# Expert results added to one row per token in DRAM, instead of two rows that are summed at the end

## The chip, the cores and the metric

The kernel runs on one core of a Trainium2 chip. The metric is the device time of one execution in microseconds (us). A core has five engines that run their own instruction streams and meet at semaphores: PE (TensorE, the matmuls; PEld is its weight load), DVE (VectorE), ACT (ScalarE), POOL (GpSimd) and SP (SyncE, which here only issues transfers). Transfers between DRAM and the on-chip memory are issued by SP, ACT or POOL and carried out by 16 DMA engines that all of them share; a transfer whose rows are picked by a list of indices (an indirect DMA) is issued by POOL.

## What is computed

The program is one layer of a decoder for 512 prompt tokens and 8 sample tokens (520 in all, 1024 features), in f32. Only its last two steps matter here: a mixture of experts, where every token goes to 2 of 32 experts, and a last RMSNorm over the residual row plus the gated sum of the two experts' outputs.

```python
def finish_layer(...):
    x = x + mods[2] * mix
    h = rmsnorm(x, norm2_g) * (1.0 + mods[4]) + mods[3]
    return x + mods[5] * hier_moe(h, ...)

# hier_moe: top-1 of 4 groups, top-2 of its 8 experts
hid = silu(einsum('nd,edf->nef', hf, w_gate)) * einsum('nd,edf->nef', hf, w_up)
y = einsum('nef,ne,efd->nd', hid, combine, w_down)
# ... and after the layer: y_prompt = rmsnorm(x, final_g)
```

## The kernel before

The program is written once, straight through; a framework turns each engine's part into one fixed instruction stream and puts in the semaphore waits that the data needs. Within an engine everything goes in order, so an instruction that waits holds back what stands behind it.

**Routing.** After the output projection each token's residual row `x1` is written to the DRAM tensor `xrow` (line 1257) and its normed row to `hrow` (line 1282). The routing code then sorts the token-expert pairs into blocks of 64 rows that share one expert. There are 36 regular blocks (`OV0`), two for each of the four fullest experts (`HV`) and one for each of the others, and 16 spare blocks (from line 1683) that this input does not need. It leaves, for every block, the list of rows to fetch (`gix`, one list for a pair of blocks), the row numbers to write to (`six`) and the weights (`wtb`).

**The block loop** (`run`, `turned`, `up`, `hidden`, `flip`, `down`). POOL gathers the rows of a pair of blocks from `hrow` into `xg` (two buffers, line 1585). PE transposes them, multiplies by the expert's gate and up weights (`pgu`, line 1608), ACT and DVE make the hidden row (`hd`, lines 1613 and 1614), PE turns it (`hTp`, line 1620) and multiplies by the down weights (`pd`, line 1629). DVE scales the result by the token's weight and the gate row into `ot`, 128 partitions by 512 (two halves of 64 rows; lines 1632 and 1633; four buffers). POOL then scatters `ot` to `yrow` with an indirect DMA (line 1634); partitions that hold no token have a row number past the end and are left out. SP streams the experts' weights, 3 MB for each, through 21 pages, which hold seven experts (line 1574). The first six experts are loaded ahead.

`yrow` has four half rows for each token, one pair for each of its two experts. No two scatters write the same row, and the program says so, so that no scatter waits for another:

```python
st = G.indirect_dma_start(out=yrow[:, :], out_offset=...six[:, b:b + 1]..., in_=ot, in_offset=None,
                          bounds_check=4 * NT - 1, oob_is_err=False)
for o in scat:
    tc.declare_no_dep(st.ins, o.ins, reason="rows of other slots")
scat.append(st)
```

**The end.** While the last blocks run, SP loads `xrow` back (`xt`, 2 MB, line 1680). After the last scatter it loads `yrow` (`yt`, eight transfers of 512 KB, line 1696, and four small ones for the sample tokens, `ysq`, line 1699). For each of four tiles of 128 tokens, DVE adds the first expert's half to `x` and then the second's (lines 1705 and 1709), ACT sums the squares (line 1710), POOL takes the power -1/2 (line 1716), DVE scales (line 1728) and SP writes the tile out (line 1729). The 8 sample tokens go a way of their own through POOL (`sample`, lines 1732 to 1734, and `quarter_rstd`, line 336) and leave by four transfers from ACT's queue (line 1746).

Of the kernel before, what the change touches and what calls it, by code (L numbers as in the profile page):

```python
# [24 lines left out]
NF = 6  # L25
# [4 lines left out]
GF_ = ()  # L30
ORD, ISS = "t0 t1 f0 t2 f1 s t3 q f2 f3", "fsq"
GT, TH, TF = (), (1, 1, 1, 2), (1, 1, 1, 2)
# [59 lines left out]
def _route():  # L92
# [7 lines left out]
    f = {"dmask": (p < NE - NF)[:, None], "half": (p // 64)[:, None] + 4 * BIG, "valid": (p < NB)[:, None],  # L100
# [80 lines left out]
def body(tc, I, O, dbg=lambda *a: None):  # L181
# [898 lines left out]
    xrow = dr.tile([SEQ, 1024], F32, name="xrow")  # L1080
    yrow = dr.tile([4 * NT, 512], F32, name="yrow")
# [142 lines left out]
    def new_rows():  # L1224
        V.tensor_scalar(pqs[:, 0], pqs[:, 0], ra[:, 0, 4:5], None, op0=ALU.mult)
# [24 lines left out]
    def project(i, n):  # L1250
# [6 lines left out]
        SP.dma_start(xrow[128 * i:128 * i + 128, 512 * n:512 * n + 512], xh)  # L1257
# [405 lines left out]
    pgus, hds, hTs_, scat = {}, {}, {}, []  # L1663
# [24 lines left out]
    ry = yrow.rearrange("(t a) f -> t (a f)", a=4)  # L1688
    ssf = cp.tile([128, 8], F32, name="ssf")
    rsf = cp.tile([128, 8], F32, name="rsf")  # L1690
    ysq = mid("ysq").rearrange("p (a f) -> p a f", a=2)
    V.memset(ysq, 0.0)
    yt = [page(f"yt{i}") for i in range(4)]
    for i in range(4):
        for j in range(2):
            SP.dma_start(half(yt[i], j), ry[128 * i:128 * i + 128, 1024 * j:1024 * j + 1024])  # L1696
        if i == 1:
            for q in range(4):
                SP.dma_start(ysq[32 * q:32 * q + 8].rearrange("p a (c j) -> p (a c) j", c=8),  # L1699
                             ry[512:520].rearrange("b (x r j) -> b x r j", r=4, j=32)[:, :, q])  # L1700
    fs = small("fs")

    def total(i):
        t, t1, x = half(yt[i], 0), half(yt[i], 1), half(xt[i // 2], i % 2)
        (G if i in GT else V).tensor_tensor(x, x, t, op=ALU.add)
        n = 1024 // TH[i]
        for h in range(TH[i]):
            c = slice(n * h, n * h + n)
            op = V.tensor_tensor(t[:, c], x[:, c], t1[:, c], op=ALU.add)  # L1709
            S.activation(t1[:, c], t[:, c], AF.Square, scale=1.0 / 32, accum_out=ssf[:, 2 * i + h:2 * i + h + 1])  # L1710
        r = rsf[:, i:i + 1]
        if TH[i] == 2:
            V.scalar_tensor_tensor(r, ssf[:, 2 * i:2 * i + 1], EPS, ssf[:, 2 * i + 1:2 * i + 2], op0=ALU.add, op1=ALU.add)
        else:
            V.tensor_scalar(r, ssf[:, 2 * i:2 * i + 1], EPS, None, op0=ALU.add)
        G.tensor_tensor(r, r, mh[:, 0:1], op=ALU.pow)  # L1716
        return op

    def final(i):
        n = 1024 // TF[i]  # L1720
        for h in range(TF[i]):
            c = slice(n * h, n * h + n)
            t = half(yt[i], 0)[:, c]
            if i in GF_:
                S.activation(t, t, AF.Copy, scale=rsf[:, i:i + 1])
                G.tensor_tensor(t, t, gfb[:, c], op=ALU.mult)
            else:
                V.scalar_tensor_tensor(t, t, rsf[:, i:i + 1], gfb[:, c], op0=ALU.mult, op1=ALU.mult)  # L1728
            SP.dma_start(O[0][0, 128 * i:128 * i + 128, c], t)

    def sample():
        G.tensor_tensor(fs, ysq[:, 0], ysq[:, 1], op=ALU.add)  # L1732
        G.tensor_tensor(fs, fs, m5s, op=ALU.mult)  # L1733
        G.tensor_tensor(fs, fs, x1s, op=ALU.add)  # L1734

    op = None
    for nm in ORD.split():
        with tc.issue_after(op.ins) if op is not None and nm[0] in ISS else ExitStack():
            r = (sample() if nm == "s" else quarter_rstd(rsf[:, 4:5], fs, 1.0 / D, EPS) if nm == "q" else
                 total(int(nm[1])) if nm[0] == "t" else final(int(nm[1])))  # L1740
        if nm[0] == "t":
            op = r
# [27 lines left out]
```

## Time and profile before

| | |
|---|---|
| median of 3 runs | 810.88 us (805.48 to 825.68) |
| the profiled execution | 803.52 us |
| its span in the trace | 801.7 us |
| block loop, first to last scatter's issue | 537.1 to 765.1 us |
| the end, from the first load of `yrow` | 769.9 to 801.7 us |
| DMA moved in all | 200.02 MB, 249 GB/s on average |

The span is the time from the first to the last instruction in the trace; 1.8 us of the profiled execution lie outside it. Busy shares are averages over the whole span; what a change in the block loop or in the end is worth has to be read in that stretch. A row of the timeline gives start and duration in us, the engine (SPq, ACTq, POOLq are sequencers, which only issue), the line, what is written and read, and in brackets how long the engine was idle before and what ended that.

### The profile page before, as it was taken

How to read it: one execution, taken by the hardware profiler on the slowest of the kernel's cores; microseconds unless marked ns; L12 is line 12 of the kernel's file. 1: busy time of each engine (PE TensorE's matmuls, PEld its weight loads, DVE VectorE, ACT ScalarE, POOL GpSimd, SP SyncE). 2: the span in 40 equal slices, each digit the busy share in tenths (PEclk: the TensorE clock that was granted, in tenths of full speed). 3: DMA queues.
4: the chain of work that ended last, by engine and by line, in shares of the span. 5: the costliest groups of instructions: out<-in, count | busy, mean ns of one | idle time of the engine just before them, and what ended most of it. 6: DMA issues, size and time to landing. Idle time of an engine off the chain costs nothing. (4 is left out here: it accounts for less than half of the span.)

```text
span 801.7 us, 12644 instructions
## 1 busy us (share of the span) xinstructions
PE 697.0 (87%) x4888; PEld 422.2 (53%) x4888; DVE 445.0 (56%) x960; ACT 214.2 (27%) x491; POOL 210.0 (26%) x182
## 2 busy tenths in 40 slices
PE   4999798997989998999999996199999999988800
PEld 3555787876767456544444553155555555545400
DVE  3444729999972868652377668833333334333235
ACT  1254721211122447643335333011011110001011
POOL 5134305043022101014361234212322222311104
PEclk9999999998988999999998999589999999999965
DMA  9975325644958502520015578479999999999653
GB/s 346 421 312 204 140 81 212 239 168 179 335 219 336 242 2 85 218 105 1 0 36 228 194 260 304 153 292 420 418 398 344 419 418 417 417 419 416 261 170 153
DMA packets 42332, 200.02 MB, mean 249 GB/s; under 512 B 10733, under 2 KB 14205, under 8 KB 22677
## 3 DMA queue, kind: packets, MB, share of 16 engines
q1 hardware_dynamic: 29341, 156.27, 50.2%
q0 software_dynamic: 10336, 40.95, 13.2%
q10 hardware_dynamic: 2592, 1.95, 0.8%
q8 instruction: 40, 0.66, 0.3%
q14 instruction: 23, 0.19, 0.1%
HBM read 187.82 MB, written 22.15 MB: 262 GB/s over the span
## 5 line engine op out<-in xcount | busy, mean ns | idle before, releaser
L591 DVE SCALAR_TENSOR_TENSOR y<-u,c,y 128x511 f32<-128x511 f32 (+23 forms) x120 | 103.7, 895 | 2.1
L1634 POOL DMA_INDIRECT yrow<-ot,six x36 | 39.5, 1098 | 107.1 <-DVE ot L1633 99.0
L1613 ACT ACTIVATE hd<-pgu 64x256 f32<-64x256 f32 x36 | 13.5, 375 | 201.1 <-PE pgu L1608 201.1
L1608 PE MATMUL pgu<-eg,mB 128*64 128x256 f32 x256 | 61.5, 383 | 0.0
L1629 PE MATMUL pd<-ed,hTe 128*64 128x512 f32 x240 | 60.3, 600 | 0.4 <-DVE hTe L225 0.4
L1608 PE MATMUL pgu<-eu,mB 128*64 128x256 f32 x256 | 60.3, 382 | 0.0
L1633 DVE SCALAR_TENSOR_TENSOR ot<-pd,wtb,mt 128x512 f32<-128x512 f32 x36 | 27.0, 751 | 54.9 <-PE pd L1629 54.9
L1608 PE MATMUL pgu<-eg,mA 128*64 128x256 f32 x224 | 53.8, 383 | 0.0
L1608 PE MATMUL pgu<-eu,mA 128*64 128x256 f32 x224 | 52.9, 382 | 0.0
L1614 DVE TENSOR_TENSOR hd<-pgu,hd 64x256 f32<-64x256 f32 x36 | 15.4, 428 | 64.8 <-ACT hd L1613 64.8
L1608 PEld LDWEIGHTS pgu<-eg,mB 128*64 128x64 f32 x256 | 33.3, 137 | 21.3 <-issue 6.4
L1608 PEld LDWEIGHTS pgu<-eg,mA 128*64 128x64 f32 x224 | 29.2, 137 | 18.6 <-issue 5.9
L1367 DVE TENSOR_REDUCE ast<-pSp 128x1 f32<-128x384 f32 (+3 forms) x44 | 26.9, 632 | 19.9 <-PE pSp L1364 19.7
L1372 ACT ACTIVATE P<-pSp,ast 128x128 f32<-128x128 f32 (+3 forms) x64 | 33.0, 528 | 15.3 <-DVE ast L1367 13.5
L370 PE MATMUL pr<-cTs,wc 128*64 128x256 f32 x256 | 37.1, 400 | 0.0
L1608 PEld LDWEIGHTS pgu<-eu,mB 128*64 128x64 f32 x256 | 33.8, 137 | 0.8
L1253 PE MATMUL woA<-wo,qT 128*128 128x512 f32 x64 | 32.1, 606 | 0.0
L1109 PE MATMUL woC<-wo,y 128*128 128x512 f32 x64 | 31.2, 605 | 0.0
L361 PE MATMUL cT<-CI,cR 128*128 128x128 f32 x128 | 21.1, 302 | 10.8 <-DVE cR L386 10.7
L1391 PE MATMUL oT<-PTp,kv 128*64 128x512 f32 x80 | 30.2, 618 | 0.0
L225 DVE COPY hTe<-hTp 128x128 f32<-128x128 f32 x36 | 10.5, 291 | 35.0 <-PE hTp L1620 33.7
L1608 PEld LDWEIGHTS pgu<-eu,mA 128*64 128x64 f32 x224 | 29.0, 137 | 0.6
(572 smaller groups left out, 1677.3 us busy)
## 6 DMA issues: line engine op xcount, KB each, us to landing
eg<-in_WG SPq DMA_DIRECT2D x26, 1024.0 KB
eu<-in_WU SPq DMA_DIRECT2D x26, 1024.0 KB
ed<-in_WD SPq DMA_DIRECT2D x26, 1024.0 KB
wada<-in_WA SPq DMA_DIRECT2D x16, 1024.0 KB
wada<-in_WA POOLq DMA_DIRECT2D x8, 1024.0 KB
WG<-in_WG SPq DMA_DIRECT2D x6, 1024.0 KB
WU<-in_WU SPq DMA_DIRECT2D x6, 1024.0 KB
WD<-in_WD SPq DMA_DIRECT2D x6, 1024.0 KB
```

The lines of the kernel that those rows point to most:

```text
L361: PE.transpose(p[:, j, :], R[b:b + n, c, k, 2 * s8:2 * s8 + 2, :], ident[b:b + n, b:b + n])
L370: mark["PE"] = PE.matmul(self.pr[r][64 * c:64 * c + 64], wc1[:, c, 8 * r + 4 * h + s, :], self.T[h][:, c, s], start=(h == 0 and s == 0), s ...
L591: V.scalar_tensor_tensor(yb[:, s_:CVS], ub[:, :CVS - s_], w(k), yb[:, s_:CVS], op0=ALU.mult, op1=ALU.add)
L1109: PE.matmul(p, zc[:, g, 128 * i:128 * i + 128], wo[2 * n + 1][:, g], start=(g == 0), stop=(g == 3))
L1253: PE.matmul(pA, oTp[:, g, 128 * i:128 * i + 128], wo[2 * n][:, g], start=(g == 0), stop=(g == 3))
L1367: V.tensor_reduce(st[k][:, 0, h0:h0 + nh], pS[k][:, :nh * L].rearrange("p (h l) -> p h l", h=nh), axis=AX.X, op=ALU.max, negate=True)
L1372: S.activation(P[k][:, g, :L], pS[k][:, o:o + L], AF.Exp, bias=st[k][:, 0, g:g + 1], accum_out=st[k][:, 1, g:g + 1])
L1391: PE.matmul(oT[64 * k:64 * k + 64, :], kv12[:, br - 1, kt, 128 + 64 * k:192 + 64 * k], PT[k], start=(br == 1 and kt == 0), stop=False)
L1608: PE.matmul(pgus[b][64 * h:64 * h + 64, :], xT[:, c, 64 * s_:64 * s_ + 64], w[:, c, :], start=(c == 0), stop=(c == 7))
L1629: PE.matmul(pd[64 * h:64 * h + 64, :], hT_[:, c, :], wd[:, c, 512 * h:512 * h + 512], start=(c == 0), stop=(c == 1))
L1633: V.scalar_tensor_tensor(ot, pd, wtb[:, b:b + 1], mt, op0=ALU.mult, op1=ALU.mult)
L1634: st = G.indirect_dma_start(out=yrow[:, :], out_offset=bass.IndirectOffsetOnAxis(ap=six[:, b:b + 1], axis=0), in_=ot, in_offset=None, boun ...
```

## The change

`yrow` gets one row of 1024 (two half rows) for each token. The residual row `x1` is written there directly, in place of `xrow`; the eight sample rows, which keep their residual on the chip, are zeroed. Every block's scatter now adds to the rows (`compute_op=ALU.add`). Two blocks can hold the same token, so the declaration that scatters do not depend on each other is gone, and each scatter waits until the last one has landed. At the end four transfers of 512 KB bring finished sums; the loads of `xt` and both additions on DVE are gone. The routing loses five small matmuls and one DVE operation (the slot's part of the row number). The sample tokens' sums move from POOL to DVE, and the last tile's power -1/2 from POOL to ACT's square root with one Newton step on DVE.

```diff
-    xrow = dr.tile([SEQ, 1024], F32, name="xrow")
-    yrow = dr.tile([4 * NT, 512], F32, name="yrow")
+    yrow = dr.tile([2 * NT, 512], F32, name="yrow")
+    ry = yrow.rearrange("(t a) f -> t (a f)", a=2)
...
+        zr = mid("zr")
+        V.memset(zr[:16], 0.0)
+        SP.dma_start(yrow[2 * SEQ:], zr[:16])
...
-        SP.dma_start(xrow[128 * i:128 * i + 128, 512 * n:512 * n + 512], xh)
+        SP.dma_start(ry[128 * i:128 * i + 128, 512 * n:512 * n + 512], xh)
...
-    for a in range(5):
-        PE.matmul(pb[:, 1, :], Rs[:, a, 1], BO[:, 0, 2 * a + 1], start=(a == 0), stop=(a == 4))
-    t6 = box(NBLK)
-    V.tensor_scalar(t6, pb[:, 1], 2.0, K("half"), op0=ALU.mult, op1=ALU.add)
-    V.scalar_tensor_tensor(six, pb[:, 0], 4.0, t6, op0=ALU.mult, op1=ALU.add)
+    V.tensor_scalar(six, pb[:, 0], 2.0, K("half"), op0=ALU.mult, op1=ALU.add)
...
-        st = G.indirect_dma_start(out=yrow[:, :], out_offset=bass.IndirectOffsetOnAxis(ap=six[:, b:b + 1], axis=0), in_=ot, in_offset=None,
-                                  bounds_check=4 * NT - 1, oob_is_err=False)
-        for o in scat:
-            tc.declare_no_dep(st.ins, o.ins, reason="rows of other slots")
-        scat.append(st)
+        G.indirect_dma_start(out=yrow[:, :], out_offset=bass.IndirectOffsetOnAxis(ap=six[:, b:b + 1], axis=0), in_=ot, in_offset=None,
+                             bounds_check=2 * NT - 1, oob_is_err=False, compute_op=ALU.add)
...
-    for i in range(4):
-        SP.dma_start(half(xt[i // 2], i % 2), xrow[128 * i:128 * i + 128])
...
     for i in range(4):
-        for j in range(2):
-            SP.dma_start(half(yt[i], j), ry[128 * i:128 * i + 128, 1024 * j:1024 * j + 1024])
+        SP.dma_start(yt[i], ry[128 * i:128 * i + 128])
...
     def total(i):
-        t, t1, x = half(yt[i], 0), half(yt[i], 1), half(xt[i // 2], i % 2)
-        (G if i in GT else V).tensor_tensor(x, x, t, op=ALU.add)
...
+        S.activation(jy, yt[i], AF.Square, scale=1.0 / 32, accum_out=s_)
+        V.tensor_scalar(s_, s_, EPS, None, op0=ALU.add)
+        if i < 3:
+            G.tensor_tensor(r, s_, mh[:, 0:1], op=ALU.pow)
+            return
+
+        t = e2.tile([128, 2], F32, name="rt2", tag="st")
+        S.activation(t[:, 0:1], s_, AF.Sqrt)
+        V.reciprocal(t[:, 1:2], t[:, 0:1])
...
+    S.activation(rsf[:, 5:6], one, AF.Sqrt)
+    for i in range(4):
+        total(i)
+        final(i)
+        if i == 1:
+            V.tensor_tensor(fs, ysq, m5s, op=ALU.mult)
+            V.tensor_tensor(fs, fs, x1s, op=ALU.add)
+            quarter_rstd(rsf[:, 4:5], fs, 1.0 / D, EPS)
```

POOL's stream in the middle of the block loop, with what each transfer waits for (`DMASW` is the landing of an earlier transfer of POOL's, `PE` and `DVE` an instruction of these engines). Before:

```order
L1585 DMA mA_3288<-hrow_2861,gix_4518 128x1024 [waits DMASW6_49,DMASW4_49,PE_49]
L1634 DMA yrow_2863<-ot_5351,six_4519 2080x512 [waits DMASW5_49,DVE_49]
L1634 DMA yrow_2863<-ot_5402,six_4519 2080x512 [waits DVE_49]
L1585 DMA mB_3289<-hrow_2861,gix_4518 128x1024 [waits DMASW7_49,DMASW1_49,PE_49]
L1634 DMA yrow_2863<-ot_5456,six_4519 2080x512 [waits DMASW0_49,DVE_49]
L1634 DMA yrow_2863<-ot_5507,six_4519 2080x512 [waits DVE_49]
```

The same place now:

```order
L1583 DMA mA_3287<-hrow_2861,gix_4520 128x1024 [waits DMASW6_49,PE_49]
L1633 DMA yrow_2862<-ot_5347,six_4521 1040x512 [waits DMASW3_49,DVE_49]
L1633 DMA yrow_2862<-ot_5398,six_4521 1040x512 [waits DMASW5_49,DVE_49]
L1583 DMA mB_3288<-hrow_2861,gix_4520 128x1024 [waits DMASW1_49,PE_49]
L1633 DMA yrow_2862<-ot_5452,six_4521 1040x512 [waits DMASW6_49,DVE_49]
L1633 DMA yrow_2862<-ot_5503,six_4521 1040x512 [waits DMASW0_49,DVE_49]
```

The order is the same: a gather, then two scatters. POOL's eight landing semaphores (`DMASW0` to `DMASW7`) are taken in turn; what a scatter waited for before was a transfer eight places back, and is now the scatter just ahead of it.

DVE's stream at the end, before (the branch is the jump past the spare blocks):

```order
L1683 UNCONDITIONAL_BRANCH x2
L1692 MEMSET ysq 128x512
L1705 TENSOR_TENSOR xt_6415<-xt_6415,yt_7282 128x1024
L1709 TENSOR_TENSOR yt_7282<-xt_6415,yt_7282 128x1024
L1705 TENSOR_TENSOR xt_6415<-xt_6415,yt_7283 128x1024
L1715 TENSOR_SCALAR rsf<-ssf 128x1
L1709 TENSOR_TENSOR yt_7283<-xt_6415,yt_7283 128x1024
L1728 SCALAR_TENSOR_TENSOR yt_7282<-yt_7282,rsf,gf 128x1024
```

And now:

```order
L1676 UNCONDITIONAL_BRANCH x2
L1684 MEMSET ysq 128x256
L1698 TENSOR_SCALAR ssf<-ssf 128x1
L1714 SCALAR_TENSOR_TENSOR yt_7272<-yt_7272,rsf,gf 128x1024
L1698 TENSOR_SCALAR ssf<-ssf 128x1
L1722 TENSOR_TENSOR fs<-ysq,m5s 128x256
L1714 SCALAR_TENSOR_TENSOR yt_7272<-yt_7272,rsf,gf 128x1024
L1723 TENSOR_TENSOR fs<-fs,x1s 128x256
```

Between two tiles' scaling (line 1714) nothing but a tile's small addition and the sample tokens' two operations is left; the additions of lines 1705 and 1709 are gone.

ACT's stream at the end, now:

```order
L1697 ACTIVATE jy,ssf<-yt_7273 128x1024
L538 ACTIVATE jks,st<-fs 128x256
L1697 ACTIVATE jy,ssf<-yt_7273 128x1024
L1704 ACT_TABLE_LOAD
L1704 ACTIVATE rt_7312<-ssf 128x1
L1728 DMA out<-fs 64x1x32 x4
```

The square root of line 1717, which stands ahead of the loop over the tiles in the code, went to the very start of ACT's stream, so that a table load stands at the end all the same, ahead of the last tile's root and of the sample tokens' four transfers.

## Rows read from the trace of the kernel before

**Rows 1.** The page: each engine's busy time in the whole span.
```profile
PE 697.0 (87%) x4888; PEld 422.2 (53%) x4888; DVE 445.0 (56%) x960; ACT 214.2 (27%) x491; POOL 210.0 (26%) x182
```

**Rows 2.** Windows: start:end, length, each engine's busy us (instructions), PE clock, DMA share, GB/s.
```profile
530.00:595.00 65.00, 65.00 (x474) 34.10 (x472) 23.19 (x46) 6.74 (x15) 16.34 (x15) 1.00 1.01 412
595.00:620.00 25.00, 25.00 (x186) 13.02 (x184) 9.08 (x18) 2.69 (x6) 6.57 (x6) 1.00 0.92 346
620.00:690.00 70.00, 69.27 (x494) 36.11 (x492) 25.20 (x50) 7.71 (x17) 18.04 (x17) 1.00 1.02 418
690.00:745.00 55.00, 48.41 (x352) 27.52 (x350) 18.18 (x34) 5.01 (x11) 11.10 (x11) 1.00 1.00 412
745.00:770.00 25.00, 15.86 (x108) 8.09 (x103) 5.50 (x11) 1.12 (x3) 3.84 (x4) 0.96 0.44 168
770.00:802.00 32.00, 0.59 (x2) 0.50 (x2) 17.13 (x21) 5.18 (x12) 9.66 (x8) 0.50 0.58 200
```

**Rows 3.** Waits, 500 to 802 us: us in total, times, longest us.
```profile
PEld pgu L1608 <- DMA ed<-in_WD: 0.5, 2, 0.3
POOL yrow L1634 <- DVE ot L1633: 99.0, 22, 6.9
```

**Rows 4.** Timeline of POOL in the block loop.
```profile
537.07 1.03 POOL L1634 DMA_INDIRECT yrow<-ot,six  x1 [0.30 <-DVE mt L1632]
...
587.78 1.00 POOL L1634 DMA_INDIRECT yrow<-ot,six  x1 [0.30 <-issue]
592.90 1.16 POOL L1634 DMA_INDIRECT yrow<-ot,six  x1 [4.12 <-DVE ot L1633]
...
600.43 1.00 POOL L1634 DMA_INDIRECT yrow<-ot,six  x1 [0.30 <-issue]
...
729.68 1.16 POOL L1634 DMA_INDIRECT yrow<-ot,six  x1 [6.89 <-DVE ot L1633]
...
765.11 0.98 POOL L1634 DMA_INDIRECT yrow<-ot,six  x1 [5.89 <-DVE ot L1633]
```

**Rows 5.** DMA queues, 730.9 to 734 us (q1: SP's, q0: POOL's): packets, MB, share.
```profile
q1 hardware_dynamic: 180, 1.30, 100.9%
```

**Rows 6.** DMA queues, 734 to 736.3 us.
```profile
q1 hardware_dynamic: 105, 0.77, 79.5%
q0 software_dynamic: 80, 0.24, 25.7%
```

**Rows 7.** DMA queues, 766.6 to 767.2 us.
```profile
q0 software_dynamic: 80, 0.03, 19.7%
```

**Rows 8.** Timeline of the end, all engines.
```profile
769.85 1.74 SPq L1696 DMA_DIRECT2D yt<-yrow  x4
771.91 2.90 SPq L1699 DMA_DIRECT2D ysq<-yrow  x4
773.98 1.23 DVE L1705 TENSOR_TENSOR xt<-xt,yt 128x1024 f32<-128x1024 f32 x1 [3.26 <-DMA yt<-yrow]
...
776.50 1.06 ACT L1710 ACTIVATE yt<-yt 128x1024 f32<-128x1024 f32 x1 [15.63 <-DVE yt L1709]
...
780.48 1.28 DVE L1728 SCALAR_TENSOR_TENSOR yt<-yt,rsf,gf 128x1024 f32<-128x1024 f32 x1
...
789.89 0.15 DVE L1715 TENSOR_SCALAR rsf<-ssf 128x1 f32<-128x1 f32 x1 [2.19 <-ACT yt L1710]
...
790.12 0.95 POOL L1716 TENSOR_TENSOR rsf<-rsf,mh 128x1 f32<-128x1 f32 x1 [1.85 <-DVE rsf L1715]
...
793.48 1.42 DVE L1728 SCALAR_TENSOR_TENSOR yt<-yt,rsf,gf 128x512 f32<-128x512 f32 x2
793.48 3.43 ACTq L1746 DMA_DIRECT2D out<-fs  x4
```

**Rows 9.** Timeline of routing and of the loop's start.
```profile
516.43 0.27 DVE L1514 TENSOR_SCALAR rt<-ptb,RC 128x52 f32<-128x52 f32 x1
...
523.20 1.28 ACT L1613 ACT_TABLE_LOAD   x1
```

More of the change, by code (lines that the diff above doesn't have):

```diff
@@ L29 @@
 KTE = "VSSSSVVSSSSSSSVSSSSVVSSS"
-GF_ = ()
-ORD, ISS = "t0 t1 f0 t2 f1 s t3 q f2 f3", "fsq"
-GT, TH, TF = (), (1, 1, 1, 2), (1, 1, 1, 2)
+TF = (1, 1, 1, 2)
 PLAN = ",c0,spread gn im sel,,,c1,k0 n cp,,,mc,,sn n3 n1 n0 n2,k1 rw,,,nq,,,,,,,,,,,,,cs,"
@@ L99, in _route @@
          "eio": full(np.arange(32)), "rev": full(64 - np.arange(32)), "thr": full(64 * np.arange(1, 9))}
-    f = {"dmask": (p < NE - NF)[:, None], "half": (p // 64)[:, None] + 4 * BIG, "valid": (p < NB)[:, None],
+    f = {"dmask": (p < NE - NF)[:, None], "half": (p // 64)[:, None] + 2 * BIG, "valid": (p < NB)[:, None],
          "inv": np.where(p < NB, 0, -1000)[:, None], "ti": full(128 * (np.arange(10) // 2) - BIG)}
@@ L1661, in run @@
         down(*before)
-    pgus, hds, hTs_, scat = {}, {}, {}, []
+    pgus, hds, hTs_ = {}, {}, {}
     asked = {0, OV0 // 2, NBLK // 2}
@@ L1677, in body @@
     SP.dma_start(gfb, I["GF"])
-    xt = [page("xt0"), page("xt1")]
-    for i in range(4):
-        SP.dma_start(half(xt[i // 2], i % 2), xrow[128 * i:128 * i + 128])
     spare = [[page(f"sg{j}"), page(f"su{j}"), page(f"sd{j}")] for j in range(3)]
@@ L1685, in body @@
         run([(b, lambda b=b: left(b - OV0)) for b in range(OV0, NBLK)], asked)
-    ry = yrow.rearrange("(t a) f -> t (a f)", a=4)
     ssf = cp.tile([128, 8], F32, name="ssf")
     rsf = cp.tile([128, 8], F32, name="rsf")
-    ysq = mid("ysq").rearrange("p (a f) -> p a f", a=2)
+    ysq = small("ysq")
     V.memset(ysq, 0.0)
-    yt = [page(f"yt{i}") for i in range(4)]
+    yt = [half(p, j) for p in (page("yt0"), page("yt1")) for j in range(2)]
+    jy = page("jy")[:, 0:1024]
     for i in range(4):
-        for j in range(2):
-            SP.dma_start(half(yt[i], j), ry[128 * i:128 * i + 128, 1024 * j:1024 * j + 1024])
+        SP.dma_start(yt[i], ry[128 * i:128 * i + 128])
@@ L1697, in body @@
         if i == 1:
             for q in range(4):
-                SP.dma_start(ysq[32 * q:32 * q + 8].rearrange("p a (c j) -> p (a c) j", c=8),
-                             ry[512:520].rearrange("b (x r j) -> b x r j", r=4, j=32)[:, :, q])
+                SP.dma_start(ysq[32 * q:32 * q + 8].rearrange("p (c j) -> p c j", c=8),
+                             ry[512:520].rearrange("b (c r j) -> b c r j", r=4, j=32)[:, :, q])
     fs = small("fs")
     def total(i):
-        t, t1, x = half(yt[i], 0), half(yt[i], 1), half(xt[i // 2], i % 2)
@@ L1705, in total @@
-        (G if i in GT else V).tensor_tensor(x, x, t, op=ALU.add)
[L1706 to L1715, printed above, removed]
@@ L1719, in final @@
+        V.scalar_tensor_tensor(t[:, 0:1], s_, t[:, 1:2], t[:, 1:2], op0=ALU.mult, op1=ALU.mult)
+        V.tensor_scalar(t[:, 0:1], t[:, 0:1], -0.5, 1.5, op0=ALU.mult, op1=ALU.add)
+        V.tensor_tensor(r, t[:, 0:1], t[:, 1:2], op=ALU.mult)
     def final(i):
@@ L1722, in final @@
             c = slice(n * h, n * h + n)
[L1723 to L1742, printed above, removed]
+            V.scalar_tensor_tensor(yt[i][:, c], yt[i][:, c], rsf[:, i:i + 1], gfb[:, c], op0=ALU.mult, op1=ALU.mult)
+            SP.dma_start(O[0][0, 128 * i:128 * i + 128, c], yt[i][:, c])
+    S.activation(rsf[:, 5:6], one, AF.Sqrt)
[6 more added lines that the diff above has]
+            quarter_rstd(rsf[:, 4:5], fs, 1.0 / D, EPS)
     V.scalar_tensor_tensor(fs, fs, rsf[:, 4:5], gfq, op0=ALU.mult, op1=ALU.mult)
```

3 lines of the change are left out of this document (1 added, 2 removed).

## The prediction

> **What bounds the kernel now.** I began with the busy shares [rows 1]: PE 87%, POOL 26%, so neither DVE's sums nor POOL look like the limit. The windows [rows 2] show where that average misleads. From 530 to 690 us PE is busy all the time; until 745 it still is for 48.4 of 55 us. This is the block loop, and it is PE's: in the waits PE's weight loads wait 0.5 us in all for the down weights, and POOL's scatter waits 99.0 us for DVE's result, never for another transfer [rows 3]. But the loop is tight in a second place. The 16 DMA engines are full (share 1.0) in three of its windows, 65 + 70 + 55 = 190 us, with one lighter window of 25 us (0.92) and a light end after 745 (0.44). The third part is the end, 770 to 802: PE does nothing, DVE is busy 17 of 32 us, and the time goes into a load, then rounds of DVE, ACT and POOL, then the last stores [rows 8].
>
> In the loop POOL issues a scatter for each block. In mid loop two blocks take 600.43 - 587.78 = 12.65 us; over the whole loop 35 intervals take 765.11 - 537.07, so a block takes 6.5 us [rows 4]. That is the number to compare a scatter's whole duration with, since the change makes scatters follow each other.
>
> **How long a scatter takes.** The trace has no row for a landing, but the queue view does nearly as well. The scatter issued at 729.68 [rows 4] has no packet in POOL's queue until 734 [rows 5]; its 80 packets go by 736.3 [rows 6]. So with full DMA engines a scatter takes up to 6.6 us from its issue, of which 3.2 (730.84 to 734) is standing behind SP's weights and 2.3 is moving among them. With idle engines the last scatter, issued at 765.11, is through by 767.2 [rows 7]: 2.1 us. Between two transfers that wait for nothing else POOL idles 0.3 us [rows 4]. A chain of scatters as they are would thus run at 6.9 us a block in the 190 loaded us and at 2.4 on idle engines. 6.9 is already more than 6.5.
>
> On a fixed cost the Trainium skill, page "DMA: Bandwidth & Descriptors", section "Anatomy of one DMA — SWDGE (gpsimd) path", gives about 2.0 us plus the bytes at 436 GB/s, which for 0.24 MB is an estimate of 2.6 us. By it the chain would be done in under half a block's time and the loop would cost nothing; the trace agrees where the engines are idle (2.1 us) and not where they are full (6.6 us).
>
> **The change part by part.**
>
> The end. In the old end the first addition starts at 773.98, 4.1 us after its load was issued at 769.85 [rows 8]; the new end has its first tile complete then. For each tile ACT's squares are 1.06 us plus a short read-out, POOL's power 0.95, DVE's scaling 1.28; handovers make it some 3.3 to 4. DVE runs in order, so a tile's small addition stands behind the last tile's scaling, and the power sits between: about 2.9 a tile. That puts the third tile's scaling at 783. The sample tokens' power and scaling (some 2 us) and the last tile's root, its four small DVE operations (0.15 each, as line 1715's) and two half scalings (1.42 together) end near 787.5. ACT's table load (1.28 [rows 9]), which the order leaves at the end, runs while DVE and POOL do the sample rows. In the old trace the last scaling ends at 793.48 + 1.42 = 794.9 and the span 6.8 us later. Keeping that, the new end is at 794.3: **7.4 us gained**, taken as 8, since 2 MB less is loaded. Bounds: 3, if each of the four rounds takes 4 us, one after the other; 13, if only the four loads and one tile's round set it. POOL no longer does the sample sums, and SP's four small loads (2.9 us of issue) still stand between the second and third tile's load, as before.
>
> Routing. One DVE operation (0.27 [rows 9]) and five small matmuls go from a path that ends in the first transposes: 0 to 0.4 us gained, 0.3 taken. Zeroing the sample rows is one DVE fill and one SP issue, tens of us before the loop, beside the projection's work. Writing `x1` into `yrow` costs what writing `xrow` did. The first scatter now waits for those stores too, but they are issued long before 537. The square root at the very start takes a table load on ACT while the first inputs come in: nothing.
>
> Loads of `xt` (2 MB) are gone from the last blocks' time, where DMA is at 0.44: nothing on the path.
>
> The scatters. Each one now reads the old row, adds and writes: 2080 half rows of 2 KB, 4.3 MB more to read, some 10 us of all 16 engines at 412 GB/s [rows 2], spread over the loop. What I cannot see in this trace is how much longer one such transfer takes. Below: nothing, if the old rows' reads pass along with the others; it can't be less than 0, since the same rows are still written. Above: as much again as the stretch in which its packets move, 2.3 us. I take 1.3, a little over half of it: about half of a block's 128 rows hold a token (2080 of 36 x 128), only these have something to read, and a sum must wait for the later of two reads. So the chain's step in loaded time is P = 6.9 + 1.3 = **8.2 us**, between 6.9 and 9.2.
>
> What stands behind the waiting scatter: on POOL the next gather, one for two blocks, and the next scatters. `ot` has four buffers, so DVE is held when a scatter is about 4 x 6.5 - 8.2 - 1 = 16 us late, and DVE then holds the hidden rows and so PE. Until then lateness costs nothing, if it can be made up. It can where the engines run empty: the last three scatters go at some 3.7 us (2.4 + 1.3) against a block's 7.1 (729.68 to 765.11, five blocks [rows 4]), which gives back about 10 us. In the loaded 190 us the chain does 190 / P blocks in place of 190 / 6.5, so the loop grows by 190 x (1 - 6.5 / P) - 10: at 8.2 that is 39.4 - 10 = **29 us**; at 6.9 it is 1; at 9.2, 46. The weights' time does not come on top: the loop is then longer than the transfers need.
>
> Sum: +29 - 8 - 0.3 = **+21 us** on the profiled execution's 803.5, so 824.5. The median of the runs shown is 7.4 us above that execution; on it the forecast is 832.
>
> **The rivals.**
>
> *The chain stays hidden* (ends on the other side: not slower). If the added reads cost nothing, P is 6.9, the loop grows by about 1 us, and what is left is the end's 8: -7, or 804 on the median's scale. It decides at P = 7.2, where growth (18.5 - 10) eats the end's gain. For it: PE is the loop's limit, the slack of four buffers, and a lighter window in mid loop. Against it: it needs an adding transfer to be as quick as a plain one.
>
> *Two full reads for each row.* The Trainium skill, page "Collectives: The Full Stack", section "The bandwidth ceiling: the fold count and why AG ≠ RS ≠ AR", says that an add inside the DMA costs nothing itself but needs two source reads on one ring, which halves the rate; its collectives are not in this trace. As a mechanism of this kernel: every packet of the scatter comes twice, so the 2.3 us of rows 6 become 4.6, P is 9.2 and the loop grows by 46: +38, or 849. That is the upper end of the forecast's own case.
>
> *The second read waits in line again.* If the old row is read only after the new one, the transfer stands a second time behind the weights (3.2 us), P = 6.9 + 3.2 + 1.3 = 11.4, and the loop grows by 82 - 10 = 72: +64, or 875. For it: nothing but the waiting time itself; against it: engines that have several packets under way.
>
> *The end gains more.* With the hidden chain and the end at its bound of 13, less the routing's 0.4, 797; over 2% would need more still.
>
> That the wait doesn't come about can be left out: the order shows every scatter waiting for the one ahead.
>
> **How the numbers follow.** Chances: the chain bounds the loop with P between 7.5 and 10 (two full reads included) 0.54; hidden 0.27; the second wait in line 0.13; a larger gain at the end 0.06. The measurement tells about 2% (16 us) from no change, so the same means 795 to 827. Faster by more holds most of the last rival, 0.05. The same holds the hidden chain and the part of the forecast with P under 7.9 (a quarter), 0.41. Slower holds the rest, 0.54. The range goes from the hidden chain with a somewhat better end, 800, to P = 10 (66 - 10 - 8 = +48, 859) with a little to spare, 862; it leaves out the second wait in line and the best end. The forecast's own range is 817 (P = 7.5) to 859.
>
> **What would show it.** Right: scatters at even distances of 8 us or more in the loaded windows, POOL waiting for the landing of `yrow` instead of for DVE, PE with gaps that end with DVE or with `xTp`, DMA share below 1 in mid loop, the last scatter at 785 to 800, and 24 to 25 us from the first load of `yrow` to the span's end. Wrong: scatters that still follow DVE at 6.3 us with the last one near 765 (P was over-priced), or distances over 10 us (a second wait). If the end does not come nearer to its first load than 29 us, its rounds, not the sums, set it.

## The result

The changed kernel takes 849.5 us in the median of four runs (847.1 to 862.0), against 812.8 for the kernel before, measured beside it: 1.052 times as long, with a 95% interval of 1.045 to 1.059. Executions of one kernel differ by 2% and more, the long ones at a lower granted TensorE clock; all ratios set those aside, so they are not quotients of the medians. Its profiled execution took 847.1 us, with a span of 845.4, 43.6 more than that of the kernel before. The forecast was 832 and its range 800 to 862.

Busy shares, from the page of the changed kernel:

```profile
PE 713.4 (84%) x4883; PEld 426.0 (50%) x4883; DVE 436.7 (52%) x957; ACT 217.4 (26%) x493; POOL 220.0 (26%) x178
```

Against [rows 1] PE gained 16 us, with five matmuls fewer, POOL 10, and DVE lost 8. Busy time doesn't show where 43.6 us went. The windows do (columns as in [rows 2]):

```profile
530.00:595.00 65.00, 65.00 (x474) 34.04 (x472) 21.72 (x43) 6.75 (x15) 13.67 (x10) 1.00 1.00 397
595.00:620.00 25.00, 20.14 (x134) 9.89 (x132) 8.02 (x16) 2.32 (x5) 6.63 (x5) 0.93 0.78 257
620.00:690.00 70.00, 58.99 (x374) 28.79 (x370) 17.64 (x35) 5.41 (x12) 15.98 (x12) 0.88 0.98 369
690.00:745.00 55.00, 42.38 (x260) 21.15 (x260) 14.67 (x29) 3.91 (x9) 14.22 (x10) 0.91 0.95 360
745.00:770.00 25.00, 12.26 (x70) 6.81 (x72) 3.82 (x8) 1.11 (x3) 6.84 (x5) 0.73 0.75 262
770.00:815.00 45.00, 39.37 (x286) 22.26 (x284) 14.40 (x28) 3.45 (x8) 13.44 (x9) 1.00 0.42 110
```

PE, which filled its windows to 690, now idles from 595 on: 11 of 70 us in the third window, half of the fifth. Where it pauses, its granted clock is lower too, 0.73 to 0.93 from 595 to 770 in place of 0.96 to 1.00: a matmul of the third window takes 158 ns where it took 140, so PE is busy longer with less to do. The DMA engines, but for 595 to 620, stay nearly full to 745 and busy to 770, where they were at 0.44 before; from 595 to 762 us their share is 0.94. The block loop has become longer, and it is no longer PE's. Whose it is, the waits say (500 to 846 us; total, times, longest):

```profile
POOL yrow L1633 <- DMA yrow<-ot,six: 150.2, 23, 9.4
DVE ot L1631 <- DMA yrow<-ot,six: 73.6, 16, 8.3
...
PE pgu L1606 <- DVE mA L223: 11.5, 4, 3.8
...
PE xTp L1596 <- DMA mB<-hrow,gix: 10.1, 1, 10.1
```

In [rows 3] the scatter waited for DVE. Now POOL waits for the landing of the scatter ahead, DVE for a free `ot` that a scatter still holds, and PE stands behind DVE and behind a gather that came late through POOL. That is the chain of the prediction. Its links, from POOL's timeline:

```profile
537.64 1.63 POOL L1633 DMA_INDIRECT yrow<-ot,six  x1 [0.30 <-DVE mt L1630]
549.43 1.58 POOL L1633 DMA_INDIRECT yrow<-ot,six  x1 [10.16 <-DVE ot L1631]
...
559.05 1.58 POOL L1633 DMA_INDIRECT yrow<-ot,six  x1 [6.67 <-issue]
...
752.47 1.55 POOL L1633 DMA_INDIRECT yrow<-ot,six  x1 [7.54 <-DMA yrow<-ot,six]
...
782.23 1.58 POOL L1633 DMA_INDIRECT yrow<-ot,six  x1 [7.73 <-DMA yrow<-ot,six]
786.70 1.55 POOL L1633 DMA_INDIRECT yrow<-ot,six  x1 [2.89 <-DMA yrow<-ot,six]
...
820.77 1.55 POOL L1633 DMA_INDIRECT yrow<-ot,six  x1 [5.31 <-DVE ot L1631]
```

From the second scatter (549.43) to the 25th (752.47) there are 23 links (a link is the time from one scatter's start to the next one's) of 8.83 us on average. They are not even: the same timeline has single ones from 4.4 to 11.0 us. In the kernel before the same stretch takes 6.39 us a block, from its timeline:

```profile
542.32 1.18 POOL L1634 DMA_INDIRECT yrow<-ot,six  x1 [4.22 <-DVE ot L1633]
...
689.21 1.00 POOL L1634 DMA_INDIRECT yrow<-ot,six  x1 [0.30 <-DVE hTe L225]
```

With the engines nearly idle a link is 786.70 - 782.23 = 4.5 us. An issue takes 1.55 to 1.73 us, where it took 1.0 to 1.2 in [rows 4].

So the 43.6 us are: the first scatter 0.6 later; the loop, first to last scatter, 283.1 in place of 228.0, **+55.1**; the landing of the last scatter, 5.4 in place of 4.7; the end, 19.2 in place of 31.9, **-12.7**. Of the loop's 55.1, the first link has 6.5 (11.8 in place of 5.3), the 23 links have 23 x 2.44 = 56.2, and the last eleven blocks give back 7.6 (68.3 in place of 75.9).

A loaded link from inside, by the queues. The scatter issued at 559.05 is through POOL at 560.63. First 560.7 to 563.7 us, then 563.7 to 567.3:

```profile
q1 hardware_dynamic: 171, 1.25, 99.3%
...
q0 software_dynamic: 13, 0.01, 0.9%
...
q1 hardware_dynamic: 199, 1.43, 94.5%
q0 software_dynamic: 144, 0.04, 7.5%
```

It stands 3 us behind SP's weights, as the scatter of [rows 5] did, and moves for 3.5 us, where that of [rows 6] took 2.3. And it has **144 packets, not 80**. The next scatter starts at 568.40, 1.1 us after the last packet.

The end, which answers to [rows 8]:

```profile
826.19 0.81 SPq L1688 DMA_DIRECT2D yt<-yrow  x2
...
830.02 1.06 ACT L1697 ACTIVATE jy<-yt 128x1024 f32<-128x1024 f32 x1 [13.49 <-DMA yt<-yrow]
...
831.44 0.57 POOL L1700 TENSOR_TENSOR rsf<-ssf,mh 128x1 f32<-128x1 f32 x1 [9.12 <-DVE ssf L1698]
832.05 1.28 DVE L1714 SCALAR_TENSOR_TENSOR yt<-yt,rsf,gf 128x1024 f32<-128x1024 f32 x1 [0.69 <-POOL rsf L1700]
...
834.17 1.28 DVE L1714 SCALAR_TENSOR_TENSOR yt<-yt,rsf,gf 128x1024 f32<-128x1024 f32 x1 [0.44 <-POOL rsf L1700]
...
836.52 1.29 DVE L1714 SCALAR_TENSOR_TENSOR yt<-yt,rsf,gf 128x1024 f32<-128x1024 f32 x1 [0.66 <-POOL rsf L1700]
...
839.82 1.41 DVE L1714 SCALAR_TENSOR_TENSOR yt<-yt,rsf,gf 128x512 f32<-128x512 f32 x2
```

The first tile is there 3.8 us after its load's issue, and tiles are scaled 2.1 and 2.4 us apart.

### The profile page after: what moved, and what is told of

The parts are those of the page before. It is cut to its first block, busy times and chain, and to the rows that moved or that the text cites. A ratio compares the mean times of both kernels' runs of the same rounds, so it can differ in the third digit from the quotient of the medians.

```text
span 845.4 us, 12621 instructions
## 1 busy us (share of the span) xinstructions
PE 713.4 (84%) x4883; PEld 426.0 (50%) x4883; DVE 436.7 (52%) x957; ACT 217.4 (26%) x493; POOL 220.0 (26%) x178
## 3 DMA queue, kind: packets, MB, share of 16 engines
HBM read 183.60 MB, written 22.18 MB: 243 GB/s over the span
## 5 line engine op out<-in xcount | busy, mean ns | idle before, releaser
L1633 POOL DMA_INDIRECT yrow<-ot,six x36 | 56.9, 1579 | 208.9 <-DMA yrow<-ot,six 150.2
L1606 PE MATMUL pgu<-eg,mA 128*64 128x256 f32 x224 | 60.1, 412 | 11.5 <-DVE mA L223 11.5
L1627 PE MATMUL pd<-ed,hTe 128*64 128x512 f32 x240 | 67.4, 669 | 0.4 <-DVE hTe L223 0.4
L1606 PE MATMUL pgu<-eg,mB 128*64 128x256 f32 x256 | 63.8, 392 | 4.5 <-DVE mB L223 4.5
L1606 PE MATMUL pgu<-eu,mB 128*64 128x256 f32 x256 | 62.1, 389 | 0.0
L1606 PE MATMUL pgu<-eu,mA 128*64 128x256 f32 x224 | 58.7, 409 | 0.0
L1612 DVE TENSOR_TENSOR hd<-pgu,hd 64x256 f32<-64x256 f32 x36 | 15.4, 428 | 62.0 <-ACT hd L1611 60.3
L1627 PEld LDWEIGHTS pd<-ed,hTe 128*64 128x64 f32 x240 | 18.8, 153 | 27.8 <-issue 24.6
L1606 PEld LDWEIGHTS pgu<-eu,mA 128*64 128x64 f32 x224 | 30.7, 145 | 1.6
```

What stands on the lines that cost most here:

```text
L1606: PE.matmul(pgus[b][64 * h:64 * h + 64, :], xT[:, c, 64 * s_:64 * s_ + 64], w[:, c, :], start=(c == 0), stop=(c == 7))
```

## The experiments

Three theories are weighed. **A**: the wait at the price of an adding transfer: each scatter waits for the last, and an adding one takes longer under load. **B**: adding transfers load the DMA engines, whether anyone waits or not. **C**: the wait alone; adding is free. The time before the loop differs by over 20 us between profiled executions (the first scatter is seen from 534 to 561 us), also between kernels whose instructions there are the same, so the stages of the traces count first and the ratios second. One table holds the stages of all kernels with 36 scatters:

| kernel | first link | links 2 to 24, each | last eleven | loop | the end | ratio to before (95%) |
|---|---|---|---|---|---|---|
| before | 5.3 | 6.39 | 75.9 | 228.0 | 31.9 | |
| after | 11.8 | 8.83 | 68.3 | 283.1 | 19.2 | 1.052 (1.045 to 1.059) |
| plain chain | 9.7 | 7.50 | 61.3 | 243.4 | 31.7 | 1.018 (1.009 to 1.026) |
| slots, adding | 5.3 | 6.30 | 82.0 | 232.3 | 27.9 | 1.005 (0.998 to 1.012) |
| after, plain | 10.2 | 7.53 | 66.1 | 249.5 | 20.7 | 1.013 (1.005 to 1.021) |
| two chains | 5.3 | 6.29 | 81.3 | 231.3 | 28.1 | 1.001 (0.995 to 1.006) |
| wide rows | 10.7 | 8.17 | 63.0 | 261.6 | 20.3 | 1.029 (1.020 to 1.039) |
| fewer weights | 7.0 | 7.50 | 54.6 | 234.1 | 18.7 | one run |
| slots, wide rows | 6.1 | 6.43 | 79.5 | 233.6 | 28.0 | 1.007 (1.003 to 1.012) |

### The wait alone: the kernel before as a plain chain

```diff
-        for o in scat:
-            tc.declare_no_dep(st.ins, o.ins, reason="rows of other slots")
-        scat.append(st)
```

> The kernel before, with plain scatters to four half rows a token, but each scatter waits for the one ahead (the declaration that they do not depend on each other is taken out). Theory A (the wait costs, at the price of an adding transfer of 144 packets): a plain transfer is shorter, scatters at about 7 us, so only 5 to 20 us over the kernel before. Rival B (it is the adding transfers' own load on the DMA engines, whoever waits): no change, within 3 us of the kernel before. Rival C (the wait alone, adding is free): the loop as long as in the changed kernel, some 55 us over the kernel before.

Measured: 827.6 us, 1.018. The loop grows by 15.4, and a loaded link takes (716.66 - 544.27) / 23 = 7.50 us. POOL's timeline:

```profile
544.27 1.01 POOL L1634 DMA_INDIRECT yrow<-ot,six  x1 [8.69 <-DVE hd L1614]
...
716.66 1.00 POOL L1634 DMA_INDIRECT yrow<-ot,six  x1 [5.29 <-DMA yrow<-ot,six]
...
767.98 0.98 POOL L1634 DMA_INDIRECT yrow<-ot,six  x1 [2.09 <-issue]
771.08 0.98 POOL L1634 DMA_INDIRECT yrow<-ot,six  x1 [2.12 <-DMA yrow<-ot,six]
```

The last two show what the prediction could not see, the way from a scatter's last packet to the next one's start. The one issued at 767.98 has its packets between 769.4 and 770.05, and from then to 771.05 all engines are empty:

```profile
q0 software_dynamic: 80, 0.11, 46.0%
...
DMA packets 0, 0.00 MB, mean 0 GB/s; under 512 B 0, under 2 KB 0, under 8 KB 0
```

A link has some 1.0 to 1.2 us after its last packet, not the 0.3 that two transfers without a wait between them leave. The wait by itself costs 15 of 55 us: C, which wanted it all here, falls. B, which wanted no change here, has missed too.

### The wait alone, from the other side: the changed kernel with plain scatters

The sums are left out; a row keeps what its last writer wrote.

```diff
-                             bounds_check=2 * NT - 1, oob_is_err=False, compute_op=ALU.add)
+                             bounds_check=2 * NT - 1, oob_is_err=False)
```

> The changed kernel with its waits, but plain scatters instead of adding ones; the sums over the experts and with the residual are left out (the last writer of a row stays). Theory A: scatters at about 7 us, the loop 5 to 20 us over the kernel before, the end 13 us shorter: 800 to 815 on a kernel before of 808. Rival B: loop as before, 793 to 797. Rival C: no faster than the changed kernel, 845 to 850.

Measured: 826.3 us, 1.013, somewhat above what A expected. Of its profiled execution only the links are read: 7.53 us, the plain chain's 7.50. With the sums left out the link loses 1.3 us. The mean granted clock was 0.912 here and 0.943 in the plain chain: PE's clock did not set these links.

### Adding without the wait: four half rows for each token, as before

```diff
-    xrow = dr.tile([SEQ, 1024], F32, name="xrow")
+    ry = yrow.rearrange("(t a) f -> t (a f)", a=4)
...
+        for i in range(4):
+            SP.dma_start(ry[128 * i:128 * i + 128, 1024:2048]..., zr...)
...
-        SP.dma_start(xrow[128 * i:128 * i + 128, 512 * n:512 * n + 512], xh)
+        SP.dma_start(ry[128 * i:128 * i + 128, 512 * n:512 * n + 512], xh)
...
-                                  bounds_check=4 * NT - 1, oob_is_err=False)
+                                  bounds_check=4 * NT - 1, oob_is_err=False, compute_op=ALU.add)
```

> Adding transfers that do not wait for each other: four half rows a token as before, so that no two scatters write the same row; the residual is written to the first expert's rows, zeros to the second's, and the end adds the two once. Theory A: the loop is within 5 us of the kernel before, the end 5 to 9 us shorter: 798 to 812 on a kernel before of 808. Rival B: the loop grows by 30 us or more: 830 and up. Rival C: as A.

Measured: 812.6 us, 1.005. The same adding transfers, with the declaration that they don't depend on each other, leave blocks at 6.30 us:

```profile
538.93 1.75 POOL L1639 DMA_INDIRECT yrow<-ot,six  x1 [3.63 <-DVE ot L1637]
...
683.92 1.76 POOL L1639 DMA_INDIRECT yrow<-ot,six  x1 [2.03 <-DVE ot L1637]
```

B falls as the cause of the change's loss. It isn't nothing, though: the last eleven blocks take 6 us more. The windows 620 to 690 and 690 to 745:

```profile
620.00:690.00 70.00, 67.90 (x486) 35.86 (x486) 25.34 (x50) 6.75 (x15) 24.71 (x17) 1.00 1.03 404
690.00:745.00 55.00, 48.07 (x352) 27.39 (x348) 17.71 (x34) 5.33 (x12) 15.88 (x10) 1.00 1.01 392
```

Engines as full as in [rows 2] move 404 and 392 GB/s in place of 418 and 412: the sums take some 3 to 5% of their time, and SP's weights come that much later. That is much for transfers so small. From 545 to 750 us POOL's queue, in the kernel before and here:

```profile
q0 software_dynamic: 4583, 7.18, 9.4%
```

```profile
q0 software_dynamic: 6556, 7.11, 15.3%
```

The same bytes, gathers included, take 1.6 times the engines' time. The end, with one addition for each tile left, is 4.0 us shorter, less than A's 5 to 9.

### Two chains

Even blocks add to `yrow`, odd ones to a second tensor that starts at zero; each chain has every second block, so a link has two blocks' time.

```diff
+        G.indirect_dma_start(out=(yrow, yro2)[b % 2][:, :], ..., in_=ot, in_offset=None,
+                             bounds_check=2 * NT - 1, oob_is_err=False, compute_op=ALU.add)
```

> The changed kernel with two accumulators: even blocks add to the rows with the residual, odd blocks to rows that begin at zero, so that each scatter waits for the last but one; one addition for each tile at the end. Theory A: two blocks (13 us) are longer than an adding transfer (9.5), the chain is hidden, the loop within 8 us of the kernel before and the end 5 to 9 us shorter: 799 to 812. Rival B: 830 and up, as the adding transfers are all still there. Rival C: as A.

Measured: 813.8 us, 1.001, blocks at 6.29 us. With two blocks' time to land in, a wait on an adding transfer costs nothing that the loop shows. It is the link against the single block that counts, as A has it. The gain at the end, 3.8 us, is less than A's 5 to 9.

### Half the packets: wide rows

The changed kernel, with `ot` as 64 rows of 4 KB. (Here and in the kernels below with such rows, the result tile lies in one of the 21 pages that otherwise hold weights.)

```diff
-        ot = mid("ot")
+        ot = half(ows[b // 2 % 2], 0)[64 * (b % 2):64 * (b % 2) + 64]
...
-        G.indirect_dma_start(out=yrow[:, :], ... six[:, b:b + 1] ..., compute_op=ALU.add)
+        G.indirect_dma_start(out=ry[:, :], ... six[0:64, b:b + 1] ..., compute_op=ALU.add)
```

> The changed kernel, still one chain of adding scatters, but a block's result lies as 64 rows of 4 KB in place of 128 of 2 KB, so a scatter has half as many rows to send and half as many row numbers to read; DVE does two scalings of 64 x 512 for each block more. The bytes written, and read for the sum, are the same. If what an adding transfer costs beyond a plain one (about 1.8 us of the 9.4 that a loaded step took) hangs on the number of rows, the step falls to 7.8 to 8.2 us, the loop grows by 25 to 32 us over that of the kernel before in place of 55, and the time is 820 to 832. If it hangs on the bytes that are read back, the step stays at 9.4 and the time at 845 to 850.

Measured: 835.1 us, 1.029; the loop grows by 33.6 in place of 55.1, a little more than expected. POOL's queue from 564.5 to 568.7, where the scatter of 561.05 lands, and POOL's timeline:

```profile
q0 software_dynamic: 80, 0.04, 5.4%
```

```profile
552.46 1.43 POOL L1635 DMA_INDIRECT yrow<-ow,six  x1 [9.21 <-issue]
...
740.40 1.56 POOL L1635 DMA_INDIRECT yrow<-ow,six  x1 [5.32 <-DMA yrow<-ow,six]
...
773.98 1.40 POOL L1635 DMA_INDIRECT yrow<-ow,six  x1 [2.77 <-DMA yrow<-ow,six]
778.22 1.40 POOL L1635 DMA_INDIRECT yrow<-ow,six  x1 [2.84 <-DVE hTe L223]
```

The same bytes go in 80 packets, as for a plain scatter, and a loaded link falls from 8.83 to 8.17. (The expectation counted a loaded link at 9.4, which is more than the mean of links 2 to 24.) Of the 1.33 us that adding puts on a loaded link, 0.66 thus go with the number of rows, as far as a kernel with a page of weights less can tell. The other 0.67 go with adding itself. On idle engines a link takes 3.1 us plain, 4.2 adding with 80 packets and 4.5 with 144: there adding itself costs 1.1 and the packets 0.3.

What adding does to the transfer shows in one block on idle engines. Plain, issued at 767.98, it is in the plain chain's view above: first packet some 1.5 us after the issue began, 80 packets within 0.65 us. Adding, in the changed kernel, it is issued at 801.58 and lies between 803.6 and 805.1:

```profile
q0 software_dynamic: 144, 0.11, 59.8%
```

POOL's longer issue lets the packets start some 0.6 us later, and they move for 1.3 us. The engines' time is 59.8% of 1.5 us, or 0.90, against 46.0% of 0.65 us, or 0.30: three times as much for the same 0.11 MB.

### Engines that aren't full: fewer weights

The changed kernel; the down weights behind the sixth expert are not loaded, the first expert's are used for them, which leaves these weights out of the result.

```diff
-        W = [page(f"eg{j}"), page(f"eu{j}"), page(f"ed{j}")]
-        for t, nm in zip(W, ("WG", "WU", "WD")):
+        W = [page(f"eg{j}"), page(f"eu{j}")]
+        for t, nm in zip(W, ("WG", "WU")):
...
-        return at(W)
+        return at(W + [ahead[0][2]])
```

> The changed kernel with its chain and 144 packets for each scatter untouched, but the down weights of all experts behind the sixth are not loaded (the first expert's are used in their place, which leaves these weights out of the result), so that a third of the loop's transfers is gone and the engines are no longer full. If the chain is slow because each link stands behind weights in the engines, a step falls to 4.5 to 6 us, less than a block's 6.5 on PE, and the loop is back at 226 to 236 us although every scatter still waits for the last. If the wait costs what it does whatever the load, the step stays at 8 us or more and the loop at 260 or more.

Measured: 807.3 us in one run, a loop of 234.1 us, with the chain and its 144 packets as they were. The loop is where it was expected. The links are not: they are 7.50 on average where 4.5 to 6 were expected, with the engines back at a share of 0.90 from 620 to 690. The trace shows both cases. Early, while the engines are nearly full (share 0.91 to 595 us), a link takes 9.5 us; late, at a share of 0.22, 4.5:

```profile
573.36 1.55 POOL L1633 DMA_INDIRECT yrow<-ot,six  x1 [7.54 <-DVE mt L1630]
...
582.83 1.58 POOL L1633 DMA_INDIRECT yrow<-ot,six  x1 [6.55 <-DVE hd L1612]
...
746.40 1.58 POOL L1633 DMA_INDIRECT yrow<-ot,six  x1 [2.56 <-DVE hd L1612]
750.88 1.55 POOL L1633 DMA_INDIRECT yrow<-ot,six  x1 [2.90 <-DVE hTe L223]
```

```profile
745.00:770.00 25.00, 25.00 (x186) 13.17 (x186) 9.17 (x18) 2.56 (x6) 7.85 (x5) 1.00 0.22 33
```

There PE is busy all 25 us again, with every scatter still waiting for the last. The price of the wait is that of standing among the weights.

### Two slots with wide rows

Two rows for each token as in the slots kernel, with rows of 4 KB, no waits, and the sample rows' loads on ACT's queue.

```diff
-        st = G.indirect_dma_start(out=yrow[:, :], ... six[:, b:b + 1] ...)
+        st = G.indirect_dma_start(out=yw[:, :], ... six[0:64, b:b + 1] ...)
...
-                SP.dma_start(ysq[32 * q:32 * q + 8]...
+                S.dma_start(ysq[32 * q:32 * q + 8]...
```

> Two rows for each token, one for each of its experts, so that no scatter waits; the first holds the residual and is added to, the second starts at zero; one addition for each tile at the end; rows of 4 KB as in the kernel of wide rows, and the sample rows are loaded from ACT's queue so that SP's four tile loads follow each other. With no chain the loop is within 3 us of that of the kernel before (228), the end is 25 to 28 us in place of 31.9, and the ratio is 0.99 to 1.00. If adding transfers are slow even where nothing waits for them, the loop is 240 or more and the ratio over 1.01.

Measured: 814.0 us, 1.007 (1.003 to 1.012): not the gain that was expected. The loop is 5.6 us longer than before and the end 28.0 us, no better than the slots kernel's 27.9. Wide rows and SP's freed queue together helped neither; which of them did what, one run with both can't say.

### Fewer links: two blocks in a scatter

```diff
+    rank = np.array([sorted(range(32), key=lambda e: (e >= NE - NF, e % 8, e // 8)).index(e) for e in range(32)])
...
+        if NF <= b < OV0:
+            ix, ot = gix[:, b // 2:b // 2 + 1], half(ows[b // 2 % 2], 0)
+        else:
+            ix = six[0:64, b:b + 1]
+        if b % 2 or not NF <= b < OV0:
+            G.indirect_dma_start(out=ry[:, :], ... ap=ix ..., in_=ot, ..., compute_op=ALU.add)
```

> The kernel of wide rows, still with every scatter waiting for the last, but from the seventh block on one scatter carries two blocks (128 rows of 4 KB), so the chain has 6 + 15 links in place of 36. The experts that get one block each are taken in another order (one of each group in turn, where the routing code ranks them), so that for these inputs the two blocks of a scatter never hold the same token; for other inputs, and for the spare blocks that these inputs don't need, that order isn't worked out. If the loop grew because a link of some 8.5 to 9.4 us stood against a block's 6.5, a link of two blocks takes about 10 to 12 us against 13: the loop is back at 228 to 238 us, the end stays at 19 to 21 in place of 31.9, and the time is 798 to 808, a ratio of 0.985 to 0.995. If a link's time grows with its rows (twice 8.5), the chain still bounds the loop at 255 or more and the time is 825 or more.

Measured: 820.6 us, 1.013 (1.006 to 1.020). The stages came out nearly as expected, the time did not. The loop is 238.1 us and the end 19.6. From 600 to 800 us the chain is hardly seen any more; POOL's wait for a scatter's landing there, against 150.2 us in the changed kernel's loop:

```profile
POOL yrow L1641 <- DMA yrow<-ow,gix: 15.9, 2, 8.0
```

Three things ate the end's 12 us: 10 in the loop, 3 in the landing of the last scatter, which is now 7.7 us, and, in the profiled execution, a first scatter at 554.8 us, 17.7 later than before. The last is no effect that I can place: the instructions ahead of the loop are the same, in the same order, as in the wide-rows kernel, which reached it at 541.8. Two further kernels look at the loop's 10.

```diff
-                                 bounds_check=NT - 1, oob_is_err=False, compute_op=ALU.add)
+                                 bounds_check=NT - 1, oob_is_err=False)
```

> The kernel of paired links with plain scatters: the sums are left out, a row keeps what its last writer wrote; every wait stays. The loop with paired links was 238.1 us, 10 more than that of the kernel before, of which the first six links, one block each at 8 to 9 us, made 10 by the eighth block and later blocks gave back 5 and lost 5 again where SP's weights set the pace. If what was lost again is the engines' time that the sums take from the weights, plain scatters give a loop of 228 to 233 and more GB/s in the full windows (405 to 418 against 366 to 406). If it is only the single links at the start, whose plain step of 7.7 us is still longer than a block's 6.3, the loop stays at 234 to 238. The time is 808 to 818 either way, since the end is the same.

```diff
-        if NF <= b < OV0:
+        if NF <= b < OV0 or b in (2, 3):
```

> The kernel of paired links with the third and fourth block in one scatter as well (these two experts share no token with these inputs), so that four links of one block are left in place of six; sums as in the kernel of paired links. If single links at the start set what was lost, the loop falls from 238.1 to 233 to 236; if the engines' time for the sums does, it stays at 237 to 239. In the kernel of paired links the stretch before the loop was 17.7 us longer than in the kernel before, with the same order of instructions there: if that comes and goes from one execution to the next, the first scatter is seen here anywhere between 534 and 561 us, as in the other runs, and the ratio is 0.995 to 1.01; if it belongs to the kernel, it is at 550 or later in both kernels of this call.

Measured: with plain scatters, and so without the sums, 801.9 us, 0.988 (0.980 to 0.997), loop 232.5, end 19.6; with one pair more 810.8 us, 0.999 (0.994 to 1.004). The windows 620 to 690 and 690 to 745, of the paired links and then of the same with plain scatters:

```profile
620.00:690.00 70.00, 69.51 (x487) 35.09 (x488) 32.82 (x59) 7.12 (x16) 15.34 (x12) 0.98 0.98 366
690.00:745.00 55.00, 48.24 (x338) 26.45 (x340) 24.47 (x43) 5.02 (x11) 11.06 (x8) 1.00 1.02 406
```

```profile
620.00:690.00 70.00, 68.85 (x488) 34.98 (x486) 33.98 (x60) 6.76 (x16) 11.97 (x11) 1.00 1.01 411
690.00:745.00 55.00, 47.51 (x338) 26.73 (x340) 22.84 (x41) 5.38 (x12) 6.59 (x6) 1.00 1.02 419
```

Plain, the loop loses 5.6 us and the full engines move more, as the theory of the engines' time had it. But the split is mixed: from the first to the seventh scatter, the single links, it takes 47.5 us in place of 53.1, all of the 5.6; of that the adding kernel regains 2 where PE sets the pace and loses 2 again where the weights do. The time of 801.9 is below the 808 to 818 expected; much of the distance to the paired links' 820.6 is ahead of the loop, where the first scatter is seen at 543.4 in place of 554.8. With one pair more it is at 559.8. Lateness that belongs to the kernel should have been at 550 or later in both of these; so it comes and goes, and why is open. The loop with one pair more, 238.8 us at a mean granted clock of 0.914, is not read. What that kernel's ratio tells is that a chain of fewer links, right for these inputs, gives back the change's whole loss and no more; why two links fewer are worth 10 us in the medians is not shown. No version was found that does the whole work in less time than the kernel before.

## Why the prediction was off

The mechanism was right: scatters over 8 us apart in the mean (though not at even distances), POOL waiting for landings, PE's gaps behind DVE and the gather, engines below full, no second wait in line (the mean link is far from 11.4). The size was not: the growth of the loop was forecast as 29 us and is 55.

**The step that failed** is the formula that turns a link's length P into the loop's growth, 190 x (1 - 6.5 / P) - 10. It counts how many blocks a chain gets done in the 190 us in which the engines were full, and lets the rest go at the pace of idle engines. But SP loads a page of weights only when a block has freed one (it waits 198 us for that in the changed kernel, 101 before), so the loaded time grows with the blocks: the share of 0.44 after 745 is now 0.75, and slow links go on to 762.6 us. If the same 29 blocks stay loaded, the growth is 190 x (P / 6.5 - 1) - 10. With the P on record, 8.2, that is 40 and not 29, which alone would have put the forecast at 843. Three chains can be held against it, each up to the end of its last slow link. The changed kernel (to 762.62, 25 links), wide rows (to 764.26, 27) and the plain chain (to 746.18, 28) are there 70, 53 and 34 us behind the kernel before at the same scatter, counted from the first. Without the 10, the mended form has 68, 49 and 29, the form on record 50, 39 and 25. What is given back after that is 15, 19 and 18 us and not 10, which is why the form on record, by two errors that cancel, meets the plain chain's whole growth (15, measured 15.4); for the changed kernel it gives 40, measured 55.1.

**P itself** was 8.83 and not 8.2, by the mended formula 18 us more. Of its two terms, the one that I couldn't see in the trace came out right: adding was taken as 1.3 and costs 8.83 - 7.50 = 1.33. That is luck in part: the working had only the packets' own stretch, and the runs show POOL's issue as well, 0.4 to 0.6 us longer, and a part that goes with the number of rows. The one that I thought I could read was short: a plain chain's link is 7.50 and not 6.9, since it was made of a scatter's time to its last packet and 0.3 us for POOL, where the plain chain shows 1.0 to 1.2 us from the last packet to the next scatter.

**The end** gained 12.7 and not 8, near the bound of 13. Last scaling to first load is 15.0 us (841.23 - 826.19) in place of the 17.6 of the working, because a round is 2.1 to 2.4 us and not 2.9: POOL's power takes 0.57 where 0.95 stood in [rows 8]. From there to the span's end it is 4.1 us and not the 6.8 that I kept. The two make 5.3 more, of which 0.6 had been taken off for rounding up to 8.

The sum: the formula 11 and P 18, which is 3 more than the loop's 55 needs, and the end 4.7 the other way. Taken in the other order, P has 11 and the formula 18.

**The rivals.** "The chain stays hidden" is refuted by the plain chain: even a plain wait does not hide, at 7.50 against 6.39. "Two full reads for each row" gave 849, the median measured, but by two errors that cancel: its P of 9.2 is longer than the 8.83 found, and its growth of 46 comes from the formula above; with the mended one it is 69. Each packet twice is not what the queue shows: 64 rows that add go in 80 packets, as many as 128 plain half rows of the same bytes, and 128 rows in 144. In the engines' time the rival was not too dear but too cheap: three times, not twice, in the block on idle engines above. The Trainium skill, page "Collectives: The Full Stack", section "The bandwidth ceiling: the fold count and why AG ≠ RS ≠ AR", puts an add in the DMA at half the rate, by its two source reads. The slots kernel's 3 to 5% does not speak against that, since POOL's queue has only a small share of the engines; no collective ran here, and what the added time consists of stays open. "The end gains more" had the end right, 12.7 against its 13, but needed the hidden chain.

## What to carry over

A declaration that transfers don't depend on each other can be worth their whole landing time: where the next one must wait, compare a link (issue, standing behind what else is queued, moving, and some 1 us until the next may start) with the time of one turn of the loop, on engines as full as they are there. If a link is longer, growth is about the number of turns times the difference (23 x 2.44 of 55 us here), for as long as what fills the engines is paced by the same turns; it isn't limited to the stretch that was full before. Two chains (1.001) gave back the loss here, two blocks in a scatter most of it or all (1.013, and 0.999 with one pair more), cheaper links only part of it (1.029).

## What the runs showed of the hardware

A scatter that adds sent 144 packets for 128 rows of 2 KB and 80 for 64 rows of 4 KB: one for each row and 16 more. The plain one of the same 128-row list sent 80, so two neighbouring half rows of a token went as one only when nothing was added. Its issue on POOL was longer too, mostly 1.55 to 1.75 us against 1.0 to 1.2 with 128 rows, and 1.4 to 1.6 with 64 adding rows. Adding cost engine time even where nobody waited for it: 0.90 us of all 16 engines in place of 0.30 for the same block, and with the engines full 404 and 392 GB/s in place of 418 and 412. The old rows' reads are not in the page's count: it has 183.60 MB read from HBM with the sums and without them.
